# New tokens' attention woven into the last convolution tiles, another buffer layout at the merge gates, and the residual's gates at the output projection

## The chip, the cores and the metric

The kernel runs on one core of one Trainium2 chip. The metric is the device time of one execution in microseconds, as the median of several runs; lower is better. Names of the engines: PE is TensorE (matrix products), DVE is VectorE, ACT is ScalarE, POOL is GpSimd, and SP is SyncE, which issues all of this kernel's transfers from one queue.

## What is computed

One layer of a decoder for a prompt of 1024 tokens and for 8 new tokens ("samples") with a cache of 256 tokens each. Cut to what matters here:

```
h = RMSNorm(x) * g_pre * (1 + scale) + shift
z = h @ w_in                       # one projection for both mixers
ya = (attention(z) * silu(za)) @ w_br_a
yb = (cb * conv3(cc * cx) * silu(cg)) @ w_br_b
ga, gb = sigmoid(merge)            # the merge gates, 2 x 1024 columns of z
o  = (ga * ya + gb * yb) @ w_out
y  = x + gate * RMSNorm(o) * g_post
```

`attention` has three branches with own keys and values (compressed, selected, window) and a gate on each. `gate` is the residual's gate, a vector per request from `w_ada`. All data are float32.

## The kernel before

Nearly every product is made of three PE passes, high part by high part, high by low and low by high (`mm`, line 106), where the low part is the value less its rounded high part (a copy on ACT or DVE, line 110 or 112, and a subtraction on DVE or POOL, line 115). Tokens lie in the free dimension: TT = 1032 columns (1024 of the prompt and 8 new ones), in 3 tiles of CH = 344 columns. The model's 1024 rows are 8 tiles of 128. Weights come through a ring `W` of three raw buffers (`wraw`) and three split ones (`wh`, `wl`).

The order of the code is the order of priority; a scheduler then orders each engine's instructions, and every engine runs its list strictly in that order. A tile of a closed pool gives its memory to the pools opened behind it on the same side ("left" or "right"), and a write to such memory waits for the last reader of what lay there, transfers included.

The stages from the middle on, with the names that matter:

- The prompt's attention (up to line 1108), with three of the four convolution tiles as filler between its products.
- The fourth convolution tile (`conv_tiles(3, ...)`, line 1120): four projections of 72 products each (cc, cx, cb, cg), evaluated by DVE, ACT and POOL.
- Branch B's projection (`w_br_b`, the loop from line 1299): 8 x 3 tiles of 12 products with 344 columns. Into it the generator `sample_steps` is woven, two steps a tile. It is the new tokens' attention: for each of the two branches over cached keys, 8 samples are loaded (`skv`), transposed on PE (`psT<-ident,skv`), split by ACT and DVE (`skT`), multiplied with the queries (`psS<-skT,qd`), put through a softmax, and multiplied with the cached values in 16 products of 8 columns (`psO<-sPT,skv`; each is two records in the trace). The same loop also makes sums of `Hh`, `Hl` for the merge gates (`sums23`).
- The `za` projection (line 1338): its end `e_za` makes `zt`, then `oh` and `ol`, which are stored to `oad` in HBM.
- The merge gates (line 1364 on): pairs of column tiles by a seven-product scheme (`a11`, `a12`, `s2`, `s3`, `s1`, `a22`, `s4`), whose weights are loaded into six buffers `ra`, summed on DVE (`wraw`), split, and multiplied. `M` receives branch B's result again (`M<-ybd`).
- Branch A's projection (`w_br_a`, loop at line 1583): 8 x 3 tiles of 12 products; DVE joins each tile with its gate (`sg`, `M`, lines 1597 and 1598). Beside it `w_out` is loaded (`wor`) and split into `WOh` (ACT) and `WOl` (half on DVE, half on POOL). After the third column tile the function `residual_gates` is called (line 1600).
- The output projection: 8 token tiles of 48 products with 512 columns, `split_m` ahead of each and `finish` behind it.

Of the kernel before, what the change touches and what calls it, by code (L numbers as in the profile page):

```python
# [29 lines left out]
NS = 8  # L30
# [55 lines left out]
def _build(ctx, tc, nc, I, O):  # L86
# [27 lines left out]
    def sub(eng, out, a, b):  # L114
        eng.tensor_tensor(out=out, in0=a, in1=b, op=OP.subtract)  # L115
# [998 lines left out]
    bctx = ExitStack()  # L1114
    bp = pool("bp", "right", bctx)
    YH = bp.tile([128, 4, TT], F32R, name="YH")
    YL = bp.tile([128, 4, TT], F32R, name="YL")
    zctx = ExitStack()
    zp = pool("zp", "left", zctx)
    y3 = zp.tile([128, TT], F32, name="y3")  # L1120
    conv3 = conv_tiles(3, y3, zp)
    for n, _ in enumerate(conv3):
        if n % 24 == 8 and n // 24 < 3:
            f = n // 24
            copy(A, YH[:, f, :], YB[f])
            sub(V, YL[:, f, :], YB[f], YH[:, f, :])
    copy(A, YH[:, 3, :], y3)
    sub(V, YL[:, 3, :], y3, YH[:, 3, :])
    pt = bank("T")
    for f in range(4):  # L1130
        PE.transpose(pt[:10, 128 * f:128 * f + 128], ucs[:, f, :], ident)
    csr = zp.tile([10, 512], F32, name="csr")
    copy(V, csr, pt[:10])
    dma(O["conv_state_prompt"][0, 0], csr[0:2, :])
    dma(O["conv_state_sample"][0, :, 1, :], csr[2:10, :])
    zctx.close()
    yctx.close()
    dram = ctx.enter_context(tc.tile_pool(name="dram", bufs=1, space=bass.MemoryType.DRAM))
    gm_d = dram.tile([18, D], F32, name="gmd")
    oa_d = [dram.tile([3, 128, 4, CH], F32, name=f"oad{i}") for i in range(2)]  # L1140
    sg_d = dram.tile([KT, 128, TT], F32, name="sgd")
    yb_d = dram.tile([KT, 128, TT], F32, name="ybd")


    HT, HS = TT // 2, TT // 4
    tsctx = ExitStack()
    tsp = pool("tsp", "left", tsctx)
    T2, T3 = ([tsp.tile([128, 4, HT], F32R, name=f"T{i}{x}") for x in "hl"] for i in (2, 3))

    def add(out, a, b):  # L1150
        V.tensor_tensor(out=out, in0=a, in1=b, op=OP.add)

    def quarter(k, c):

        cs = slice(HT * c, HT * c + HT)
        return Hh[:, k, cs], Hl[k][:, cs]

    def two(h, l, src):
        copy(A, h, src)
        sub(V, l, src, h)  # L1160

    def sums23(tp):
        for k in range(4):
            for s in range(2):
                cs = slice(HS * s, HS * s + HS)

                def part(k, c):
                    return [x[:, cs] for x in quarter(k, c)]

                a, b = (tp.tile([128, HS], F32, name=x, tag=x, bufs=1) for x in ("ta", "tb"))  # L1170
                add(a, *part(k + 4, 1))
                add(b, *part(k, 1))
                sub(V, a, a, b)
                two(T3[0][:, k, cs], T3[1][:, k, cs], a)
                yield
                add(b, *part(k, 0))
                add(b, a, b)
                two(T2[0][:, k, cs], T2[1][:, k, cs], b)
                yield


    sctx = ExitStack()
    sp = pool("smp", "left", sctx)
# [105 lines left out]

    def branch_mm(acc, w, Xh, Xl, cs):  # L1290
        wh, wl = w
        for k in range(4):
            mm(acc, wh[:, k, :], Xh[:, k, cs], k == 0, False)
            mm(acc, wh[:, k, :], Xl[:, k, cs], False, False)
            mm(acc, wl[:, k, :], Xh[:, k, cs], False, k == 3)

    steps = sample_steps()
    making = sums23(sp)
    for f in range(KT):
        w = W.get()  # L1300
        for c in range(3):
            acc = bank("acc" if (3 * f + c) % 5 < 2 else "S")[:, :CH]
            cs = slice(c * CH, (c + 1) * CH)
            branch_mm(acc, w, YH, YL, cs)
            yb = sp.tile([128, CH], F32, name="yb", tag="yb", bufs=2)
            copy(A, yb, acc)
            dma(yb_d[f, :, cs], yb)
            next(steps, None)
            next(steps, None)
            if f > 1:  # L1310
                next(making, None)
        W.release()
    for _ in steps:
        pass
    sctx.close()
    bctx.close()
# [5 lines left out]
    tp = pool("tp", "left", tctx)  # L1322
    t1 = tp.tile([128, 4, HT], F32, name="t1")

# [13 lines left out]
    for j in range(4):  # L1338
        def e_za(c, acc, cs):
            t = tp.tile([128, CH], F32, name="zt", tag="zt", bufs=3)  # L1340
            oh = tp.tile([128, CH], F32R, name="oh", tag="oh", bufs=2)
            ol = tp.tile([128, CH], F32R, name="ol", tag="ol", bufs=2)
# [22 lines left out]
    gp = pool("gsp", "left", gctx)  # L1365

# [8 lines left out]
    class Pair:  # L1375
# [63 lines left out]
        def after(self, x, s, ps):  # L1439
            def tmp(name, bufs=2):  # L1440
                return gp.tile([128, HS], F32, name=name, tag=name, bufs=bufs)
# [26 lines left out]
        def end(self, i, c, s, z):  # L1468

            f, cs = self.f + i, slice(HT * c + HS * s, HT * c + HS * s + HS)  # L1470
            if self.gb:
                t = gp.tile([128, HS], F32, name="ct", tag="ct", bufs=5)
                A.activation(t, z, AF.Tanh, scale=0.5)
                V.scalar_tensor_tensor(M[:, f, cs], t, 1.0, M[:, f, cs], op0=OP.add, op1=OP.mult)
                return
            if i == 0 and c == 0 and s == 0:
                self.sg = [gp.tile([128, TT], F32, name="sgo", tag="sgo", bufs=2) for _ in range(2)]
                self.left = [4, 4]
# [4 lines left out]

    gm = gp.tile([18, D], F32, name="gm")
# [75 lines left out]
    def residual_gates():  # L1560
        gm = op_.tile([19, D], F32, name="gm2")
        dma(gm[0:18, :], gm_d)
        dma(gm[18:19, :], I["b_ada"][:, 2048:3072])
        gs2 = op_.tile([51, D], F32R, name="gs2")
        kr = op_.tile([51, 136], F32R, name="kr")
        V.memset(f32(gs2), 0.0)
        copy(V, kr, ksel[:, 9:145])
        copy(A, gs2[0:19, :], gm)
        sub(V, gs2[32:51, :], gm, gs2[0:19, :])
        gps = op_.tile([128, D], F32, name="gps")  # L1570
        src = I["g_post"]
        dma(gps, bass.AP(tensor=src.tensor, offset=src.offset, ap=[[0, 128], [1, D]]))
        V.tensor_scalar(gps, gps, float(D) ** 0.5, None, op0=OP.mult)
        for b in range(2):
            cs = slice(512 * b, 512 * b + 512)
            ps = bank("T")
            mm(ps, kr[:, 0:128], gs2[:, cs], True, True)
            V.tensor_tensor(out=GG[:, cs], in0=ps, in1=gps[:, cs], op=OP.mult)
            ps = bank("T")
            mm(ps[:NS, :], kr[:, 128:136], gs2[:, cs], True, True)  # L1580
            V.tensor_tensor(out=GS[:, cs], in0=ps[:NS, :], in1=gps[:NS, cs], op=OP.mult)

    for f in range(KT):
        sg = op_.tile([128, TT], F32, name="sg", tag="sg", bufs=3)
        dma(sg, sg_d[f])
        for h in range(2):
# [4 lines left out]
            sub(P if h else V, WOl[f][:, cs], r, WOh[:, f, cs])  # L1591
# [8 lines left out]
        if f == 2:  # L1600
            residual_gates()
# [48 lines left out]

    mt, xt = {}, {}
# [25 lines left out]
    split_m(0)  # L1677
    for t in range(8):
# [44 lines left out]
```

## Time and profile before

| | |
|---|---|
| median of 3 runs (lowest to highest) | 1083.23 us (1078.26 to 1083.63) |
| the profiled execution | 1082.31 us, its span 1080.5 us |
| mean granted clock of PE over the span | 0.976 of full speed |
| busy share of the span | PE 96%, DVE 67%, ACT 50%, POOL 10% |
| DMA | 104.16 MB, 96 GB/s over the span |
| chain that ended last | PE 76%, DVE 10%, DMA 4%, ACT 4%, rest 6% |

The span runs from the first to the last instruction; what lies around it is the 1.8 us between the two times of the profiled execution. Since PE is busy nearly throughout, its busy share alone tells little: what is to be looked for are stretches in which it waits or in which its granted clock is below 1.00. Matmul records overlap, so the distance between two starts is what a product costs, and not its length.

### The profile page before, as it was taken

The numbers are of one execution on the slowest core, as the hardware profiler recorded it, in microseconds if no ns is written. First come the engines' busy times: TensorE is split into PE (matmuls) and PEld (weight loads), VectorE is DVE, ScalarE is ACT, GpSimd is POOL, SyncE is SP. The second block draws the span as 40 slices with busy tenths as digits, with TensorE's granted clock in tenths as the row PEclk, the third lists the DMA queues.
The fourth block names the chain that finished last, engine by engine and source line by source line (L and its number), as shares of the span: only waits on it lengthen the run. The fifth ranks groups of instructions, "written<-read, shape, count | busy, mean of one in ns | idle before, by whom it ended". The sixth has DMA issues, their size and how long they took to land.

```text
span 1080.5 us, 18059 instructions
## 1 busy us (share of the span) xinstructions
PE 1033.0 (96%) x6526; PEld 950.1 (88%) x6526; DVE 729.0 (67%) x1912; ACT 545.3 (50%) x1198; POOL 105.4 (10%) x106
## 2 busy tenths in 40 slices
PE   5899999999999999999999999998999999999997
PEld 4689999988888889988999989997899999988786
DVE  4676755368877988878878485294656676794433
ACT  4566533358888877887775042232344444222221
POOL 2100000122221211211110000000000000121000
PEclk9999999989999999999999998898999999999999
DMA  9753243211110101111002226335734423773222
GB/s 322 220 143 90 71 101 79 70 35 39 28 30 16 30 15 26 25 25 26 12 18 79 72 92 209 107 112 187 244 109 119 118 69 113 245 226 99 79 79 78
DMA packets 117179, 104.16 MB, mean 96 GB/s; under 512 B 25443, under 2 KB 101674, under 8 KB 117090
## 3 DMA queue, kind: packets, MB, share of 16 engines
q1 hardware_dynamic: 117090, 103.02, 32.3%
q8 instruction: 51, 0.84, 0.3%
q14 instruction: 38, 0.31, 0.1%
HBM read 79.13 MB, written 21.76 MB: 93 GB/s over the span
## 4 chain that ended last, share of the span: by engine, by line
PE 76%; DVE 10%; DMA 4%; ACT 4%; issue 2%; SPq 1%; POOL 1%; POOLq 0%; DVEq 0%; ACTq 0%
PE psacc L106 35%; PE psS L106 22%; PE psO L106 6%; PE psT L1016 5%; PE psT L106 5%; DVE P L961 2%; DVE P L987 2%; ACT P L966 1%; SPq L91 1%; DVE pl L115 1%; DMA sg<-sgd 1%; ACT ph L110 1%; PE psT L1028 1%; DMA ar<-w_ada 1%; DVE sm L975 1%
## 5 line engine op out<-in xcount | busy, mean ns | idle before, releaser
L106 PE MATMUL psacc<-Hh,wh 128*128 128x344 f32 (+1 forms) x816 | 261.7, 321 | 8.9 <-ACT c L110 5.0
L106 PE MATMUL psacc<-Hl,wh 128*128 128x344 f32 (+1 forms) x816 | 258.6, 317 | 0.8 <-DVE ss L329 0.6
L106 PE MATMUL psacc<-Hh,wl 128*128 128x344 f32 (+1 forms) x816 | 258.1, 318 | 0.1
L106 PEld LDWEIGHTS psacc<-Hh,wh 128*128 128x128 f32 x816 | 155.1, 190 | 17.1 <-ACT c L110 5.2
L106 PEld LDWEIGHTS psacc<-Hl,wh 128*128 128x128 f32 x816 | 154.9, 190 | 5.7 <-DVE Hl L115 2.2
L106 PEld LDWEIGHTS psacc<-Hh,wl 128*128 128x128 f32 x816 | 154.5, 190 | 2.4 <-DVE wl L115 1.1
L966 ACT ACTIVATE P<-P,mx 128x64 f32<-128x64 f32 (+5 forms) x192 | 115.1, 600 | 34.7 <-DVE mx L961 32.9
L115 DVE TENSOR_TENSOR pl<-psT,ph 128x512 fp32r<-128x512 f32 x132 | 90.4, 687 | 24.6 <-ACT ph L110 24.1
L110 ACT ACTIVATE wh<-wraw 128x512 fp32r<-128x512 f32 x94 | 58.9, 627 | 79.7 <-PE psS L106 37.0
L1016 PE MATMUL psT<-ident,P 128*128 128x128 f32 x528 | 89.5, 280 | 9.3 <-DVE P L987 7.1
L115 DVE TENSOR_TENSOR wl<-wraw,wh 128x512 fp32r<-128x512 f32 x98 | 67.3, 688 | 41.2 <-ACT wh L110 39.5
L110 ACT ACTIVATE ph<-psT 128x512 fp32r<-128x512 f32 x132 | 77.9, 591 | 28.6 <-PE psT L1016 24.5
L961 DVE CUSTOM_DVE_ANT_0 P<-psS,kbig 128x64 f32<-128x64 f32 (+4 forms) x192 | 74.2, 407 | 20.2 <-PE psS L106 19.4
L1016 PEld LDWEIGHTS psT<-ident,P 128*128 128x128 f32 x528 | 63.6, 141 | 26.9 <-DVE P L987 10.9
L106 PE MATMUL psS<-K,qh 128*128 128x384 f32 (+6 forms) x208 | 67.7, 328 | 2.0 <-DMA qh<-qh 1.1
L106 PE MATMUL psS<-K,ql 128*128 128x384 f32 (+6 forms) x208 | 68.5, 330 | 0.0
L115 POOL TENSOR_TENSOR wl<-wraw,wh 128x512 fp32r<-128x512 f32 x28 | 37.1, 1325 | 275.0 <-ACT wh L110 262.9
L106 PE MATMUL psO<-pl,V 128*128 128x512 f32 x132 | 60.7, 460 | 0.0
L106 PE MATMUL psO<-ph,V 128*128 128x512 f32 x132 | 52.4, 397 | 0.0
L961 DVE CUSTOM_DVE_ANT_0 P<-psS,kbig,mx 128x256 f32<-128x256 f32 (+3 forms) x80 | 41.9, 524 | 9.3 <-PE psS L106 8.3
L115 POOL TENSOR_TENSOR WOl<-wor,WOh 128x512 fp32r<-128x512 f32 x8 | 11.6, 1445 | 342.2 <-ACT WOh L110 338.2
L106 PEld LDWEIGHTS psS<-K,qh 128*128 128x128 f32 x208 | 39.6, 190 | 4.8 <-DMA qh<-qh 1.4
(393 smaller groups left out, 2374.3 us busy)
## 6 DMA issues: line engine op xcount, KB each, us to landing
wraw<-w_in SPq DMA_DIRECT2D x46, 256.0 KB
ra<-w_in SPq DMA_DIRECT2D x32, 256.0 KB
ybd<-yb SPq DMA_DIRECT2D x24, 172.0 KB
M<-ybd SPq DMA_DIRECT2D x8, 516.0 KB
sgd<-sgo SPq DMA_DIRECT2D x8, 516.0 KB
OA<-oad SPq DMA_DIRECT2D x6, 688.0 KB
sg<-sgd SPq DMA_DIRECT2D x8, 516.0 KB
x<-x_prompt SPq DMA_DIRECT2D x8, 512.0 KB
```

Of the source, the lines that this page charges most:

```text
L91: return nc.sync.dma_start(out, in_)
L106: PE.matmul(out, lhsT, rhs, start=start, stop=stop, skip_group_check=True)
L110: A.activation(out, in_, AF.Copy)
L115: eng.tensor_tensor(out=out, in0=a, in1=b, op=OP.subtract)
L961: V.tensor_tensor_reduce(out=Pb[:, j, o:o + n], in0=ps[:, c0:c0 + n], in1=m, scale=1.0, scalar=init, op0=OP.add, op1=OP.min, accum_out=mx[ ...
L966: A.activation(Pb[:, j, 0:total_n], Pb[:, j, 0:total_n], AF.Exp, bias=mx[:, j, ci % 2:ci % 2 + 1], scale=-1.0, accum_out=sm[:, 0, x, j:j + 1])
L975: V.tensor_tensor(out=fac, in0=fac, in1=gt_[:, b0:b0 + np_, :], op=OP.mult)
L987: V.tensor_scalar(p, p, f[:, jj:jj + 1], None, op0=OP.mult)
L1016: PE.transpose(pt[:, j * 128:(j + 1) * 128], u.P[u.br][:, j, n * 128:(n + 1) * 128], ident)
L1028: PE.transpose(pt[:64, j * 128:(j + 1) * 128], u.P[0][:, j, :], ident)
```

## The change

1. `sample_steps` is defined ahead of the fourth convolution tile, and its pool moves to the right side. One step runs at every fourth yield of the convolution's projections (24 of its 39 parts); the rest runs in branch B's loop, one step a tile instead of two.
2. At the merge gates, the buffers `oh`, `ol` and `zt` of the `za` projection are placed first in their pool, and the gate pool places `gm`, `sgo`, `c1`, `u2`, `u3`, `ct` first and `ra` behind them, so that other buffers lie over each other.
3. `residual_gates` is called behind `split_m(0)` at the output projection, and its tiles lie in that stage's pool.
4. All low parts of `w_out` are made on DVE.

```diff
@@ the fourth convolution tile @@
-    bctx = ExitStack()
...
     sctx = ExitStack()
-    sp = pool("smp", "left", sctx)
+    sp = pool("smp", "right", sctx)
...
+    steps = sample_steps()
+    bctx = ExitStack()
...
     for n, _ in enumerate(conv3):
+        if n % 4 == 3:
+            next(steps, None)
         if n % 24 == 8 and n // 24 < 3:
...
@@ branch B @@
-    steps = sample_steps()
-    making = sums23(sp)
+    t23ctx = ExitStack()
+    tp = pool("tp23", "left", t23ctx)
+    making = sums23(tp)
...
             dma(yb_d[f, :, cs], yb)
             next(steps, None)
-            next(steps, None)
...
@@ za @@
     tp = pool("tp", "left", tctx)
+    zt = {x: [tp.tile([128, CH], d, name=x, tag=x, bufs=b) for _ in range(b)] for x, d, b in
+          (("oh", F32R, 2), ("ol", F32R, 2), ("zt", F32, 3))}
     t1 = tp.tile([128, 4, HT], F32, name="t1")
...
@@ merge gates @@
     gp = pool("gsp", "left", gctx)
+    gm = gp.tile([18, D], F32, name="gm")
+    fresh = {"sgo": [gp.tile([128, TT], F32, name="sgo", tag="sgo", bufs=2) for _ in range(2)]}
+    for x, b in (("c1", 2), ("u2", 2), ("u3", 2), ("ct", 5)):
+        fresh[x] = [gp.tile([128, HS], F32, name=x, tag=x, bufs=b) for _ in range(b)]
...
@@ branch A @@
-            sub(P if h else V, WOl[f][:, cs], r, WOh[:, f, cs])
+            sub(V, WOl[f][:, cs], r, WOh[:, f, cs])
...
-        if f == 2:
-            residual_gates()
...
@@ output projection @@
     def residual_gates():
-        gm = op_.tile([19, D], F32, name="gm2")
+        gm = ob.tile([19, D], F32, name="gm2")
...
     split_m(0)
+    residual_gates()
     for t in range(8):
```

What this does to the order of the instructions is shown at three places.

PE, the products of the new tokens' probabilities with the cached values (`psO<-sPT,skv`) of the first branch. Before, in branch B's loop (`YH`, `YL` are branch B's operands):

```order
L106 MATMUL psacc<-YH,wl 128x344
L106 MATMUL psO<-pn,vnew 128x64
L106 MATMUL psO<-sPT,skv 128x8 x16
L106 MATMUL psacc<-YH,wh 128x344
L106 MATMUL psacc<-YL,wh 128x344
```

Now, in the fourth convolution tile (12 products with 344 columns lie between this group of four and the next, and so on up to the fourth):

```order
L106 MATMUL psacc<-Hh,wl 128x344
L106 MATMUL psO<-pn,vnew 128x64
L106 MATMUL psO<-sPT,skv 128x8 x4
L106 MATMUL psacc<-Hh,wh 128x344
L106 MATMUL psacc<-Hl_280,wh 128x344
...
L106 MATMUL psacc<-Hh,wl 128x344
L106 MATMUL psO<-sPT,skv 128x8 x4
L106 MATMUL psacc<-Hh,wh 128x344
```

The sixteen products that stood in one run now stand in four groups; the second branch's, which stood in two groups of eight within branch B's loop, stand in four there as well.

SP, the first loads of the merge gates, with what each waits for (`DMAHW` with a number is one of eight counters of transfers, used in turn). Before:

```order
L91 DMA M<-ybd 128x1032 [waits DMAHW5_49]
L91 DMA ra<-w_in 128x4x128 [waits DMAHW6_49]
L91 DMA ra<-w_in 128x4x128 [waits DMAHW2_49,DMAHW7_49,DMAHW0_49,Pool_49]
L91 DMA ra<-w_in 128x4x128
L91 DMA ra<-w_in 128x4x128 [waits DMAHW1_49]
```

Now:

```order
L91 DMA M<-ybd 128x1032 [waits DMAHW5_49]
L91 DMA ra<-w_in 128x4x128 [waits DMAHW6_49,PE_49]
L91 DMA ra<-w_in 128x4x128 [waits DMAHW7_49]
L91 DMA ra<-w_in 128x4x128 [waits DMAHW0_49]
L91 DMA ra<-w_in 128x4x128 [waits DMAHW1_49]
```

The loads stand at the same place of the queue. The second no longer waits for counter 2, which belongs to the last store of `oh` (`oad<-oh`) three rows ahead of the first of these loads.

PE, the residual's gates (`psT<-gs,kr`). Before, in branch A's loop (`OA` is its operand):

```order
L106 MATMUL psT<-gs_11034,kr 128x512
L106 MATMUL psT<-gs_11034,kr 8x512
L106 MATMUL psS<-OA_10675,wl 128x344
L106 MATMUL psT<-gs_11034,kr 128x512
L106 MATMUL psT<-gs_11034,kr 8x512
L106 MATMUL psS<-OA_10761,wh 128x344
```

Now, in the second token tile of the output projection:

```order
L106 MATMUL psS<-WOh,mh 128x512
L106 MATMUL psT<-gs_11356,kr 128x512
L106 MATMUL psT<-gs_11356,kr 8x512
L106 MATMUL psS<-WOl_10836,mh 128x512
...
L106 MATMUL psS<-WOl_10837,mh 128x512
L106 MATMUL psT<-gs_11356,kr 128x512
L106 MATMUL psS<-WOh,ml 128x512
L106 MATMUL psS<-WOh,mh 128x512
L106 MATMUL psT<-gs_11356,kr 8x512
```

The four products, which nothing but one product of branch A parted, now stand apart between products of the output projection, behind its first token tile.

## Rows read from the trace of the kernel before

**Rows 1.** Windows of 5 us in branch B's loop: length, engines' busy time (instructions), PEclk, DMA share, GB/s.
```profile
630.00:635.00 5.00, 5.00 (x35) 4.74 (x34) 4.55 (x14) 2.40 (x7) 0.00 (x0) 1.00 0.41 135
...
650.00:655.00 5.00, 5.00 (x31) 4.24 (x29) 4.01 (x12) 1.45 (x4) 0.00 (x0) 0.84 0.53 135
655.00:660.00 5.00, 5.00 (x23) 5.00 (x23) 0.00 (x0) 0.00 (x0) 0.00 (x0) 0.50 0.81 283
660.00:665.00 5.00, 5.00 (x24) 4.94 (x23) 2.60 (x8) 0.84 (x2) 0.00 (x0) 0.63 0.96 312
...
680.00:685.00 5.00, 5.00 (x37) 4.72 (x35) 0.69 (x2) 1.37 (x3) 0.00 (x0) 0.92 0.70 190
685.00:690.00 5.00, 5.00 (x21) 5.00 (x21) 0.42 (x2) 0.00 (x0) 0.00 (x0) 0.50 0.10 35
690.00:695.00 5.00, 5.00 (x30) 5.00 (x30) 1.12 (x2) 1.09 (x3) 0.00 (x0) 0.90 0.11 35
```

**Rows 2.** Chain that ended last, fourth convolution tile and branch B: start, length, engine, tile, line.
```profile
581.89 41.16 PE psacc L106 x262
...
652.11 6.37 PE psO L106 x34
...
684.14 3.08 PE psO L106 x16
```

**Rows 3.** Timeline of PE around products of 8 columns: start, length, instruction.
```profile
680.98 1.95 PE L106 MATMUL psO<-sPT,skv 128*128 128x8 f32 x16
682.79 0.40 PE L106 MATMUL psS<-YH,wl 128*128 128x344 f32 x1
683.03 0.32 PE L106 MATMUL psS<-YH,wh 128*128 128x344 f32 x1
```

**Rows 4.** Instructions on tile `skT`: shortest, median and longest in ns, first and last start.
```profile
L110 ACT ACTIVATE skT<-psT x16: 376/385/390, 633.8 to 674.8; 128x256 fp32r<-128x256 f32 x16
L115 DVE TENSOR_TENSOR skT<-psT,skT x16: 410/418/425, 634.4 to 675.3; 128x256 fp32r<-128x256 f32 x16
```

**Rows 5.** Timeline of DVE at the fourth convolution tile's start.
```profile
583.57 1.23 DVE L115 TENSOR_TENSOR YL<-YB,YH 128x1032 fp32r<-128x1032 f32 x1
```

**Rows 6.** Chain that ended last, from `za` into the merge gates.
```profile
746.78 4.02 DMA oad<-oh
...
751.37 5.32 DMA ra<-w_in
```

**Rows 7.** Timeline of SP (its DMA queue) at the same place.
```profile
747.71 1.00 SPq L91 DMA_DIRECT2D M<-ybd  x2
748.76 5.94 SPq L91 DMA_DIRECT2D ra<-w_in  x6
```

**Rows 8.** Timeline of ACT and a window (columns as in rows 1) at the same place.
```profile
751.45 0.66 ACT L110 ACTIVATE c<-psacc 128x258 f32<-128x258 f32 x2 [4.69 <-DMA oad<-ol]
...
750.00:755.00 5.00, 3.11 (x14) 3.11 (x15) 0.00 (x0) 0.79 (x3) 0.00 (x0) 0.50 1.09 369
```

**Rows 9.** Timeline of PE in branch A around the residual's gates; in brackets idle time and releaser.
```profile
952.27 0.48 PE L106 MATMUL psS<-OA,wh 128*128 128x344 f32 x2
952.98 0.73 PE L106 MATMUL psT<-gs,kr 51*128 51x512 f32 x2 [0.23 <-DVE gs L115]
...
957.38 0.94 PE L106 MATMUL psS<-OA,wh 128*128 128x344 f32 x2 [1.91 <-DVE sg L1597]
...
960.84 0.48 PE L106 MATMUL psacc<-OA,wh 128*128 128x344 f32 x2
```

**Rows 10.** Groups of DVE's instructions in branch A (925 to 978 us): busy, mean ns, idle before.
```profile
L115 DVE TENSOR_TENSOR WOl<-wor,WOh 128x512 fp32r<-128x512 f32 x8 | 5.5, 684 | 1.2 <-ACT WOh L110 1.1
```

**Rows 11.** Timelines of POOL, DVE and ACT in branch A.
```profile
949.10 1.49 POOL L115 TENSOR_TENSOR WOl<-wor,WOh 128x512 fp32r<-128x512 f32 x1 [4.41 <-ACT WOh L110]
...
949.36 1.52 DVE L112 CAST wh<-wraw 128x512 fp32r<-128x512 f32 x1
...
966.18 0.63 ACT L110 ACTIVATE WOh<-wor 128x512 fp32r<-128x512 f32 x1 [3.94 <-DMA wor<-w_out]
```

More of the change, by code (lines that the diff above doesn't have):

```diff
@@ L1111, in _build @@
     att.close()
-    bctx = ExitStack()
[L1115 to L1179, printed above, removed]
@@ L1288, in sample_steps @@
                  os_[r].rearrange("p (s h) -> p s h", h=8)[:, :, 4 * g:4 * g + 4])
+    steps = sample_steps()
+    bctx = ExitStack()
+    bp = pool("bp", "right", bctx)
+    YH = bp.tile([128, 4, TT], F32R, name="YH")
+    YL = bp.tile([128, 4, TT], F32R, name="YL")
+    zctx = ExitStack()
+    zp = pool("zp", "left", zctx)
+    y3 = zp.tile([128, TT], F32, name="y3")
+    conv3 = conv_tiles(3, y3, zp)
+    for n, _ in enumerate(conv3):
+        if n % 4 == 3:
+            next(steps, None)
+        if n % 24 == 8 and n // 24 < 3:
+            f = n // 24
+            copy(A, YH[:, f, :], YB[f])
+            sub(V, YL[:, f, :], YB[f], YH[:, f, :])
@@ new lines, in _build @@
+    copy(A, YH[:, 3, :], y3)
+    sub(V, YL[:, 3, :], y3, YH[:, 3, :])
+    pt = bank("T")
+    for f in range(4):
+        PE.transpose(pt[:10, 128 * f:128 * f + 128], ucs[:, f, :], ident)
+    csr = zp.tile([10, 512], F32, name="csr")
+    copy(V, csr, pt[:10])
+    dma(O["conv_state_prompt"][0, 0], csr[0:2, :])
+    dma(O["conv_state_sample"][0, :, 1, :], csr[2:10, :])
+    zctx.close()
+    yctx.close()
+    dram = ctx.enter_context(tc.tile_pool(name="dram", bufs=1, space=bass.MemoryType.DRAM))
@@ new lines, in _build, with add @@
+    gm_d = dram.tile([18, D], F32, name="gmd")
+    oa_d = [dram.tile([3, 128, 4, CH], F32, name=f"oad{i}") for i in range(2)]
+    sg_d = dram.tile([KT, 128, TT], F32, name="sgd")
+    yb_d = dram.tile([KT, 128, TT], F32, name="ybd")
+    HT, HS = TT // 2, TT // 4
+    tsctx = ExitStack()
+    tsp = pool("tsp", "left", tsctx)
+    T2, T3 = ([tsp.tile([128, 4, HT], F32R, name=f"T{i}{x}") for x in "hl"] for i in (2, 3))
+    def add(out, a, b):
+        V.tensor_tensor(out=out, in0=a, in1=b, op=OP.add)
@@ new lines, in quarter, with two, sums23, part @@
+    def quarter(k, c):
+        cs = slice(HT * c, HT * c + HT)
+        return Hh[:, k, cs], Hl[k][:, cs]
+    def two(h, l, src):
+        copy(A, h, src)
+        sub(V, l, src, h)
+    def sums23(tp):
+        for k in range(4):
+            for s in range(2):
+                cs = slice(HS * s, HS * s + HS)
+                def part(k, c):
+                    return [x[:, cs] for x in quarter(k, c)]
+                a, b = (tp.tile([128, HS], F32, name=x, tag=x, bufs=1) for x in ("ta", "tb"))
+                add(a, *part(k + 4, 1))
+                add(b, *part(k, 1))
+                sub(V, a, a, b)
+                two(T3[0][:, k, cs], T3[1][:, k, cs], a)
+                yield
+                add(b, *part(k, 0))
+                add(b, a, b)
+                two(T2[0][:, k, cs], T2[1][:, k, cs], b)
+                yield
@@ L1314, in _build @@
         pass
+    t23ctx.close()
+    bctx.close()
     sctx.close()
-    bctx.close()
     tsp4 = pool("tsp4", "left", tsctx)
@@ L1322, in _build, with spare @@
     tp = pool("tp", "left", tctx)
+    zt = {x: [tp.tile([128, CH], d, name=x, tag=x, bufs=b) for _ in range(b)] for x, d, b in
+          (("oh", F32R, 2), ("ol", F32R, 2), ("zt", F32, 3))}
     t1 = tp.tile([128, 4, HT], F32, name="t1")
+    def spare(name, dtype, bufs):
+        return zt[name].pop(0) if zt[name] else tp.tile([128, CH], dtype, name=name, tag=name, bufs=bufs)
     def sums14():
@@ L1440, in tmp @@
             def tmp(name, bufs=2):
-                return gp.tile([128, HS], F32, name=name, tag=name, bufs=bufs)
+                return gtile(name, HS, bufs)
             def total(a, b):
@@ L1471, in end @@
             if self.gb:
[L1472 removed]
+                t = gtile("ct", HS, 5)
                 A.activation(t, z, AF.Tanh, scale=0.5)
@@ L1476, in end @@
             if i == 0 and c == 0 and s == 0:
-                self.sg = [gp.tile([128, TT], F32, name="sgo", tag="sgo", bufs=2) for _ in range(2)]
+                self.sg = [gtile("sgo", TT, 2) for _ in range(2)]
                 self.left = [4, 4]
```

51 lines of the change are left out of this document (25 added, 26 removed).

## The prediction

> **What bounds the kernel now.** Four views were read, in this order. The page says that PE is busy 96% of the span and carries 76% of the chain that ended last, so a change can gain only where PE stands or runs at a lower granted clock. The windows over the span came next: PEclk is below 1.00 in a few places, and two of them lie in branch B's loop, where PE does not stand at all [rows 1]. The chain of waits then gives the price of one product and names what held PE at the merge gates [rows 2, 6]. Last, the timelines around these places show which instruction the engines were held by [rows 3, 5, 7 to 9, 11].
>
> One price serves throughout: 262 products of 344 columns took 41.16 us, so one costs 0.157 us at the full clock [rows 2].
>
> **Part A, the new tokens' attention.** In branch B's loop the granted clock was 1.00 while transposes, small products and large ones were mixed (630 to 635), fell to 0.50 in 655 to 660, and again in 685 to 690; PE was busy 5.00 of 5 us throughout [rows 1]. That is the lower of the two levels, 1.2 in place of 2.4 GHz. What PE did just before each fall is in the chain: 34 records of 6.37 us from 652.11, and 16 of 3.08 us from 684.14, all products of 8 columns on `psO` [rows 2]. So I read runs of these tiny products as what lowers the clock. The cost: in each window of 5 us the work lost is 5 x (1 - PEclk), that is 0.80 + 2.50 + 1.85 for the first fall and 0.40 + 2.50 + 0.50 for the second, together 8.55 us [rows 1].
>
> The change takes the first run of 34 records apart into four groups of 8, with 12 large products between them, and the second branch's two runs of 16 likewise. A group of 8 takes about 8 x 0.113 = 0.9 us (16 records began at 680.98 and the next product at 682.79), ahead of 12 x 0.157 = 1.88 us of large products [rows 2, 3]. That looks like the mixture of 630 to 635, which kept 1.00 [rows 1]. I therefore take the whole 8.55 us as gained. Against it stand the breaks between the two kinds of product: the first large product behind a run lasted 0.24 us to the next start, against 0.157, so a break costs about 0.08 us on that side and, by estimate, as much on the other; eight groups in place of three runs are 5 more, at 0.2 us 1.0 us [rows 3]. Net 7.5 us. The bounds: nothing of the clock comes back and the breaks remain, -1; all of it and no price for breaks, 9.
>
> What is only moved and costed at nothing: 24 of 39 steps with their loads, transposes and copies. PE's products are as many as before. The loads of cached keys and values leave SP's queue some 40 us earlier; in 655 to 665 the queue ran at a DMA share of 0.81 to 0.96 and PE still did not stand [rows 1], so weights of the convolution should not come late. The cover of a step is the 12 large products between its transposes and the products that need them, 1.88 us; ACT's 0.385 and DVE's 0.418 us for `skT` make 0.80 of it [rows 4], which leaves 1.08 us for what stands ahead of them on DVE. If that cover is gone, PE stands before each step (the last rival).
>
> The Trainium skill, page "TensorE: Matmul & The Clock Gate", section "Why this matters for your kernels", says that drops of throughput in the middle of a kernel come from idle stretches of PE between bursts of products, and to keep PE fed. By that rule alone the clock should not have fallen at 655, where the trace has no idle time, and rearranging busy work would return nothing. The row differs from it, and the row decides; what the sum would be by the rule is the first rival's 1078.0.
>
> **Part B, the merge gates.** The chain ran through the store `oad<-oh` (from 746.78, 4.02 us) and then the load of `ra` from 751.37 [rows 6]. The second `ra` load waited for that store, since it overlaid `oh`; SP's queue had the first at 748.76, right behind the loads of `M` [rows 7]. In the new layout that wait is gone, and the second load could leave at about 749.2 instead of 751.37: 2.2 us. But in 750 to 755 the DMA share was already 1.09, so an earlier issue partly shares the same bandwidth [rows 8]. ACT's copy `c`, which waited 4.69 us for the other store, no longer waits, but PE was held by `ra` for longer, so this alone gives nothing [rows 6, 8]. The bounds are 0 and 2.2; I take 1.6, nearer the issue time, because the store's wait ended the chain.
>
> **Part C, branch A and the output projection.** Ahead of the residual's gates, two products of branch A began at 952.27, so the next would have begun at 952.59. From there to the product at 960.84 lie 13 products of branch A; at 0.157 us they end at 954.6, and 6.2 us were lost [rows 2, 9]. In them are two short pairs of the residual's own products, a stand of 1.91 us for DVE's `sg`, and a stretch at the lower clock behind it, where two products last 0.94 instead of 0.48 us [rows 9]. The four products do not vanish: at 0.73 us a pair they cost 1.5 us at the output projection [rows 9], where their operands have a whole token tile of products as cover. That leaves 4.7 us.
>
> The low parts of `w_out` go the other way. POOL's half took 1.49 us for one, and a DVE cast beside it 1.52 [rows 11], against 0.684 us for DVE's own subtraction of the same size [rows 10]. On DVE the other half adds 8 x 0.684 = 5.5 us of work, and it stands in DVE's queue behind `WOh`, whose 8 present waits cost 1.2 us [rows 10]; `WOh` itself stood 3.94 us for `wor` [rows 11]. What is queued behind such a wait is the join of a tile with its gate, for which PE has already been seen to wait. DVE also loses the residual's own operations here and the stretching by POOL, so I charge PE only 1.0 us, close to the 1.2 of the present half. Net 3.7 us; the bounds are 0 (all of it goes to waits for DVE) and 5.5 (4.7 plus the smaller stretch of DVE's casts).
>
> **The sum.** 7.5 + 1.6 + 3.7 = 12.8 us off the profiled execution's 1082.3 (span 1080.5 and 1.8 around it) is 1069.5. The median of the runs shown is 1083.2, 0.9 above that execution.
>
> **The rivals.**
> - *The clock falls all the same.* If any mixture with tiny products lowers it, the first part gives -1.0 and the time is 1082.3 + 1.0 - 1.6 - 3.7 = 1078.0; if only one of the two passages falls, about 1074. For it: the fall came with PE fully busy, so I cannot show from one kernel how many tiny products are too many. Against: 630 to 635 stood at 1.00 with transposes between the large products [rows 1]. Chance 0.18: 0.10 for both, 0.08 for one.
> - *DVE becomes the bound of branch A.* With all low parts behind `wor` and `WOh` on one engine in strict order, `sg` and the weights' casts come late and part C gives nothing: 1073.2. For it: the waits of 1.2 and 3.94 us [rows 10, 11]. Against: DVE loses the residual's work. Chance 0.08.
> - *The loads at the merge gates are limited by bandwidth.* The share of 1.09 speaks for it [rows 8]; the chain's wait for a store against it [rows 6]. Part B gives 0: 1071.1. Chance 0.06.
> - *Slower: PE stands before the keys' products in the convolution.* DVE works strictly in order, and there it also has the convolution's own work, such as `YL` with 1.23 us [rows 5]. From 1.08 us of queue ahead of `skT` on, PE stands; with 2.3 us ahead at each of 16 steps [rows 4] it is 16 x 1.2 = 19.2 us, and the time 1088.7. For it: one `YL` alone exceeds the margin. Against: there are three of them for 16 steps, and in 630 to 635, with DVE busy 4.55 of 5 us, PE did not stand [rows 1]. Chance 0.07.
>
> **How the numbers follow.** The forecast keeps 0.61. A measurement of this kernel can tell about 0.5%, 5.4 us, from no change. Faster by more (below 1077.8): the forecast, the one-passage case, the second and third rival, 0.83, less 0.02 for smaller gains of several parts at once, 0.81. Within: both passages fall, 0.10, and those 0.02, with 0.01 of the slower rival in weak form, 0.13. Slower: 0.06. The range of 8 in 10 goes from 1064 (9 + 2.2 + 5.5 would be 1065.6, with 1.6 for the scatter between runs) up to 1078, which takes in three of the rivals and the edge of the first.
>
> **What would show it.** Right: PEclk at 1.00 in every window of the convolution's last tile and branch B; records on `psO` in groups of 8 and none at twice the length; no idle time of PE ahead of `psS<-skT`; the second `ra` load right behind the first; no stand at `psT<-gs` and no lower clock around it in branch A; the same products at the output projection without a wait. Wrong: PEclk of 0.50 again behind the groups of tiny products; PE waiting for DVE's `skT` in the convolution; PE waiting for `sg` or `wl` while DVE waits for `WOh`; the first seven-product group starting as late as before.

## The result and the profile after

The changed kernel takes **1070.85 us** (median of 4 runs, 1070.16 to 1071.64) against 1083.37 for the kernel before (4 runs, 1078.26 to 1083.63). The ratio is 0.9894, with a 95% interval of 0.9868 to 0.9920. The profiled execution took 1071.21 us, its span is 1069.2 us, and PE's mean granted clock rose from 0.976 to 0.986. The forecast was 1069.5.

So that the parts can be judged apart, the span is cut at starts of PE's products that every kernel has: the last `psO<-pl,V` of the prompt's attention, the last product with `YH` or `YL` (end of branch B), the first `psS<-T2h` (the first `s2`), the first with `OA` (branch A), the first `WOh,wh` and the last with `WO` (output projection). In us, profiled executions:

| stretch | before | after | difference |
|---|---|---|---|
| fourth convolution tile and branch B | 117.01 | 108.02 | -8.99 |
| `za`, up to the first `s2` | 60.64 | 61.36 | +0.72 |
| merge gates | 166.43 | 167.12 | +0.69 |
| branch A | 52.52 | 45.40 | -7.12 |
| output projection | 96.31 | 98.92 | +2.61 |

The stretch ahead of these came out 0.7 us longer in this one execution, and what lies behind the last product is unchanged; together they make the 11.4 us between the two spans (1080.54 and 1069.17 us).

Windows of the changed kernel around the places where the small products now stand (columns as in [rows 1]):

```profile
620.00:625.00 5.00, 5.00 (x38) 5.00 (x37) 0.36 (x1) 0.00 (x0) 0.00 (x0) 1.00 0.75 207
625.00:630.00 5.00, 5.00 (x38) 5.00 (x38) 0.51 (x1) 0.46 (x1) 0.93 (x1) 1.00 0.87 277
...
660.00:665.00 5.00, 5.00 (x35) 4.45 (x33) 3.58 (x11) 1.30 (x4) 0.00 (x0) 1.00 0.36 105
665.00:670.00 5.00, 5.00 (x38) 5.00 (x38) 3.96 (x10) 1.94 (x5) 0.00 (x0) 1.00 0.49 126
```

The number to read is PEclk, the third from the end: it is 1.00 in all of them, and in every other window of 5 us from 580 to 740, where [rows 1] had 0.50 twice. PE was busy 5.00 of 5 us in these windows and in those; its busy share alone could not have told the two apart. PE does not wait for `skT` anywhere from 582 to 690, but it stands 1.3 us there for branch B's operand `YH` and the probabilities `sP` (total in us, times, longest), where the kernel before has one stand of 0.3:

```profile
PE psacc L106 <- ACT YH L110: 0.7, 1, 0.7
PE psT L1161 <- DVE sP L1155: 0.6, 2, 0.4
```

The instructions on the tile `psO` of the changed kernel (shortest, median and longest in ns, first and last start) say the same of the products themselves:

```profile
L106 PE MATMUL psO<-sPT,skv x64: 170/256/277, 619.3 to 671.0; 128*128 128x8 f32 x64
```

None is as long as those that ran at the lower clock before (median 361 ns there). The chain that ended last, at the merge gates (start, length, engine, tile, line), answers to [rows 6]:

```profile
738.82 1.73 PE psacc L106 x12
...
741.71 7.43 DMA ra<-w_in
...
751.30 0.80 PE psS L106 x2
```

The wait for the store `oad<-oh` is gone from the chain, as intended, but the load of `ra` behind it now takes 7.43 us from its issue, where it took 5.32. SP's queue shows what stands ahead of it:

```profile
738.51 0.32 SPq L91 DMA_DIRECT2D oad<-oh  x1
739.07 0.32 SPq L91 DMA_DIRECT2D oad<-ol  x1
739.44 1.01 SPq L91 DMA_DIRECT2D M<-ybd  x2
740.54 6.59 SPq L91 DMA_DIRECT2D ra<-w_in  x6
```

As before [rows 7], the six loads of `ra` stand right behind loads of `M`, of 516 KB each. What PE waits for from 725 on (total in us, times, longest) and the windows at the place:

```profile
PE psS L106 <- ACT wh L110: 9.3, 1, 9.3
PE psacc L106 <- ACT c L110: 0.2, 1, 0.2
```

```profile
740.00:745.00 5.00, 1.97 (x17) 1.75 (x15) 0.00 (x0) 0.66 (x2) 0.00 (x0) 1.00 0.99 349
745.00:750.00 5.00, 0.00 (x0) 0.00 (x0) 0.80 (x2) 0.00 (x0) 0.00 (x0) 0.65 1.19 306
750.00:755.00 5.00, 3.70 (x17) 3.70 (x18) 3.97 (x7) 1.75 (x3) 0.00 (x0) 0.50 0.89 256
755.00:760.00 5.00, 5.00 (x37) 5.00 (x37) 3.01 (x7) 0.91 (x2) 0.00 (x0) 0.82 0.77 267
```

Before, PE stood 5.0 us for ACT's `c` and 2.1 for `wh`, with the products of `a12` between. Now `c` comes at once, `a12` runs at once, and the whole wait is one stand of 9.3 us, after which PE begins again at 0.50.

That list of waits holds nothing from branch A: no `sg`, no `gs`, no `GG`. The chain there is PE's alone:

```profile
918.58 3.87 PE psacc L106 x24
922.45 5.69 PE psS L106 x36
928.14 3.76 PE psacc L106 x24
...
960.20 3.78 PE psS L106 x24
```

24 products in 3.76 to 3.78 us is the full rate of 0.157 each, where [rows 9] had a stand and a stretch at the lower clock. DVE's groups between 918 and 964 show what it carries for that (busy, mean ns, idle before; the sixteenth subtraction lies just behind the stretch):

```profile
L115 DVE TENSOR_TENSOR WOl<-wor,WOh 128x512 fp32r<-128x512 f32 x15 | 10.2, 688 | 2.3 <-ACT WOh L110 2.3
```

Its waits for `WOh` doubled with the number of subtractions, from 1.1 [rows 10] to 2.3 us, and PE waited for none of it.

### The profile page after: what moved, and what is told of

It is laid out like the page before. It is cut to its first block, busy times and chain, and to the rows that moved or that the text cites. A ratio compares the mean times of both kernels' runs of the same rounds, so it can differ in the third digit from the quotient of the medians.

```text
span 1069.2 us, 18057 instructions
## 1 busy us (share of the span) xinstructions
PE 1021.5 (96%) x6526; PEld 940.3 (88%) x6526; DVE 727.9 (68%) x1920; ACT 545.6 (51%) x1198; POOL 94.0 (9%) x98
## 4 chain that ended last, share of the span: by engine, by line
PE 77%; DVE 10%; ACT 4%; issue 2%; DMA 1%; SPq 1%; POOL 1%; POOLq 0%; DVEq 0%; ACTq 0%
PE psacc L106 36%; PE psS L106 23%; PE psO L106 6%; PE psT L106 5%; PE psT L1016 5%; DVE P L961 2%; DVE P L987 2%; ACT P L966 1%; DVE pl L115 1%; SPq L91 1%; DMA ra<-w_in 1%; ACT ph L110 1%; PE psT L1028 1%; DVE sm L975 1%; PE psT L570 1%
## 5 line engine op out<-in xcount | busy, mean ns | idle before, releaser
L1613 POOL TENSOR_TENSOR fst<-fst,mhalf 128x1 f32<-128x1 f32 (+1 forms) x9 | 4.9, 549 | 422.5 <-DVE fst L1612 422.5
```

The source lines that it names most:

```text
L1613: P.tensor_tensor(out=st[:n, 3:4], in0=st[:n, 3:4], in1=mhalf[:n], op=OP.pow)
```

## The experiments

All are compared with the kernel before, run beside them on the same chip; its median there was 1081.7 to 1082.4. The columns are the stretches of the table above, from the profiled execution.

| kernel | median, us | ratio to before (95%) | conv., B | to `s2` | gates | A | output |
|---|---|---|---|---|---|---|---|
| only A | 1071.22 | 0.9896 (0.9872 to 0.9920) | 108.04 | 60.53 | 165.00 | 51.92 | 96.31 |
| only B | 1082.40 | 1.0002 (0.9989 to 1.0015) | 117.01 | 60.48 | 166.61 | 49.60 | 96.31 |
| only C | 1078.55 | 0.9970 (0.9958 to 0.9982) | 116.96 | 60.68 | 166.52 | 45.37 | 98.92 |
| C, low parts half on POOL | 1078.24 | 0.9963 (0.9948 to 0.9979) | 117.01 | 61.06 | 166.28 | 45.78 | 98.92 |
| A and C | 1070.60 | 0.9905 (0.9876 to 0.9933) | 108.03 | 60.66 | 164.93 | 46.53 | 98.91 |
| one run a branch | 1073.12 | 0.9917 (0.9892 to 0.9943) | 110.72 | 60.84 | 166.41 | 45.72 | 98.91 |
| two runs a branch | 1068.03 | 0.9877 (0.9851 to 0.9903) | 107.52 | 60.56 | 166.07 | 45.40 | 98.92 |
| spread only | 1079.45 | 0.9974 (0.9959 to 0.9990) | 115.80 | 60.52 | 164.97 | 52.09 | 96.31 |
| `M` late | 1066.50 | 0.9862 (0.9836 to 0.9888) | 108.04 | 56.73 | 166.18 | 45.68 | 98.92 |
| `M` late, old order of B | 1066.73 | 0.9863 (0.9846 to 0.9881) | 108.04 | 57.03 | 164.89 | 45.73 | 98.98 |
| `M` late, two runs, other pool | 1066.94 | 0.9875 (0.9857 to 0.9892) | 107.52 | 57.13 | 166.33 | 46.14 | 99.45 |
| `M` late, two runs, `ra` in `M` | 1066.96 | 0.9852 (0.9830 to 0.9873) | 112.23 | 56.66 | 167.19 | 45.39 | 98.91 |

### One part at a time

The edits are the hunks of the change, by part: A the convolution and branch B, B `za` and the merge gates, C branch A and the output projection.

**Only A.** 

> Only part A (new tokens' attention begun in the fourth convolution tile), merge gates, branch A and output projection as before. Theory: part A is worth what the trace of the changed kernel gave between the end of the prompt's attention and the start of za, 8.3 to 9.0 us, whatever the other parts do: about 1074.7 us, PEclk 1.00 in every window of branch B's loop, and the stand at the merge gates as before (4.98 and 2.09 us of PE). Rival: part of that gain comes from the new buffer order (shorter queues behind it), then A alone gives clearly less than 7.5 us: above 1076.

The stretch is 8.97 us shorter, the same as in the whole change, but the run is 3.5 us faster than expected: 1071.2. In the profiled execution PE's second stand at the merge gates was 1.2 us (2.1 before), and the gates were 1.4 us shorter. The windows show that the clock was back by 750 and stayed:

```profile
740.00:745.00 5.00, 2.12 (x10) 2.12 (x11) 0.00 (x0) 0.66 (x2) 0.00 (x0) 0.72 1.04 378
745.00:750.00 5.00, 3.77 (x19) 3.47 (x18) 2.36 (x4) 1.81 (x4) 0.00 (x0) 0.59 1.19 310
750.00:755.00 5.00, 5.00 (x42) 4.81 (x41) 4.84 (x10) 1.36 (x3) 0.00 (x0) 1.00 0.95 290
```

Before, the clock had come back and fell once more:

```profile
755.00:760.00 5.00, 2.91 (x18) 2.59 (x17) 3.16 (x5) 2.40 (x5) 0.00 (x0) 0.84 1.08 293
760.00:765.00 5.00, 5.00 (x33) 5.00 (x33) 3.60 (x8) 0.63 (x1) 0.00 (x0) 0.73 0.96 312
```

Branch A is 0.6 us shorter, with 2.1 us of stands in place of 3.2; the stand of 1.9 us for `sg` is still there. So part A alone is as fast as the whole change (1071.22 against 1070.85), as far as the intervals can tell.

**Only B.** 

> Only part B (buffer order at za and the merge gates). Theory: the loads at the merge gates are held by the DMA engines and not by the wait for the store, so the first product of s2 comes 0.7 us later behind the last oad<-oh (12.8 instead of 12.1 us) and PE, which now stands in one piece of 9.3 us, starts again at the lower clock and loses some 0.7 us more; branch A gets back up to 1 us since the loads of sg no longer wait for the store of gm. In all between 1082 and 1085, no gain to be told. Rival (the prediction's own step): s2 starts 1.6 us sooner, 1081.8.

1082.4: no difference. `s2` began neither later nor 1.6 us sooner (60.48 against 60.64), so both theories missed its start by size; the chain shows the load of `ra` at 6.69 us from its issue where the kernel before had 5.32. The 2.9 us less in branch A belong to this execution, in which the clock stayed at 1.00 behind the stand for `sg`; the medians are equal.

**Only C.** 

> Only part C (residual's gates at the output projection, all low parts of w_out on DVE). Theory: branch A runs without a stand (24 products in 3.76 to 3.78 us throughout), which is 7.2 us sooner at the output projection, and that stage is 2.7 us longer (2.0 for the residual's products in three places, 0.7 for products of 512 columns at 0.2334 in place of 0.2313 us): 4.5 us, 1078.9. Rival: part of branch A's gain belongs to part B, because sg's loads still wait for the store of gm here; then PE stands for sg or OA in branch A, and the gain is 2.5 to 3.5 us, 1080 to 1081.

1078.55, as the theory had it: in the profiled execution branch A is 7.15 us shorter and the output projection 2.61 longer. PE waits for nothing in branch A although the buffer order is the old one, so the rival falls.

**The move of the residual's gates without the other half of C.** The edit to the run before:

```diff
-            sub(V, WOl[f][:, cs], r, WOh[:, f, cs])
+            sub(P if h else V, WOl[f][:, cs], r, WOh[:, f, cs])
```

> Only the move of the residual's gates; the low parts of w_out stay half on POOL. Theory: the move alone takes away the stand at psT<-gs and sg, the split on POOL costs only DVE's stretched operations, which branch A can hide: within 1 us of the run with both (about 1079 to 1080), the output projection again 2.7 us longer. Rival: POOL's subtractions are what makes DVE late in branch A; then PE still waits for sg or wl there and the gain is under 2 us, 1081.5 or more.

1078.24, and branch A 45.78 in place of 45.37: which engine makes the low parts is worth 0.4 us at most and nothing in the median. The gain of C is the move.

**A and C.** 

> Parts A and C without B. Theory: B is a loss once A is there; without it the start of s2 and the gates take what the run with A alone showed (60.5 and 165.0 us in place of 61.4 and 167.1), and branch A and the output projection what the run with C alone showed (45.4 and 98.9 us): about 3 us under the changed kernel, 1067 to 1068. Rival: the 2.9 us belong to a chance of the one profiled run (the clock recovering in time or not), and A and C together are the changed kernel's time, 1070 to 1071.

The profiled execution is 1.9 us under that of the changed kernel, but the median, 1070.60, is the same: B is worth nothing that can be told, with A or without it. The 2 us at the gates are again the clock coming back sooner, as with only A; the profiled execution is the fastest of the four, which went from 1069.19 to 1073.85 (the changed kernel's from 1070.16 to 1071.64). C, too, is worth less behind A than alone. From only A to A and C, branch A is 5.4 us shorter and not 7.15: 0.6 had gone with A already, and PE stands 0.9 us for `OA` here. Less the 2.6 at the output projection this is 2.8 us, but the medians differ by 0.6 (1071.22 and 1070.60), and their intervals, of some 3 us to each side, allow either.

### What lowered the clock

**One run a branch.** In `sample_steps`:

```diff
-                if s % 2:
+                if s == NS - 1:
                     yield
```

> The changed kernel, but the 16 products of 8 columns of a branch stand again in one run (32 records) in place of four groups of 8 records; everything else stays where the change put it. Theory: it is the run that lowers the clock. PEclk falls to 0.50 behind the run in the convolution and behind the one in branch B's loop, at some 5 us each as at 650 to 665 before, less 1.2 us for six breaks fewer: 1079 to 1080. Rival: the fall belonged to the place in branch B's loop (or to its loads), not to the run; then PEclk stays 1.00 and the time is 1069.7 to 1071.

1073.12 us, some 6 less than expected, but the clock fell behind each of the two runs (34 records in the chain: 32 of 8 columns and two of 64):

```profile
619.16 4.03 PE psO L106 x34
...
657.19 4.03 PE psO L106 x34
```

```profile
620.00:625.00 5.00, 5.00 (x39) 5.00 (x39) 0.49 (x1) 0.00 (x0) 0.00 (x0) 0.93 0.70 226
625.00:630.00 5.00, 5.00 (x25) 5.00 (x25) 0.66 (x3) 0.46 (x1) 0.23 (x1) 0.73 0.90 301
...
660.00:665.00 5.00, 5.00 (x27) 5.00 (x28) 2.73 (x8) 0.67 (x2) 0.00 (x0) 0.68 0.00 0
665.00:670.00 5.00, 5.00 (x33) 5.00 (x32) 3.79 (x10) 1.77 (x6) 0.00 (x0) 0.98 0.46 125
```

So the run does it, in the convolution as in branch B; the rival falls. But the loss is 0.35 + 1.35 + 1.60 + 0.10 = 3.4 us where the same two branches lost 8.55 before. The run alone, in this place, does not bring back the whole of part A.

**Spread only.** The kernel before, with one line more:

```diff
                 if s % 2:
                     yield
+                    yield
```

> The kernel before, with nothing moved into the convolution, but two yields behind every four products of 8 columns. The order that comes of it: the second branch's products stand in four groups of 8 records with 8 to 12 large products between them; the first branch's in one group of 24 records and, 12 large products later, one of 8. Theory: spreading is what keeps the clock, not the place. Behind the second branch PEclk stays 1.00 (3.4 us of 8.55 gained); behind the group of 24 it falls or not, which no run has shown yet: 1079 if it falls, 1074 if not. Rival: work that is short of large products in branch B's loop lowers the clock wherever the small ones stand; then both falls are there again and the time is 1082.

1079.45 us. Behind the first group (24 records) PE ran at 0.50 throughout 655 to 665. The second branch, for which the theory had 1.00, still lost 0.45 + 1.25:

```profile
655.00:660.00 5.00, 5.00 (x21) 5.00 (x22) 0.20 (x1) 0.19 (x1) 0.00 (x0) 0.50 0.69 193
660.00:665.00 5.00, 5.00 (x21) 5.00 (x21) 3.76 (x9) 0.88 (x2) 0.00 (x0) 0.50 0.39 142
...
685.00:690.00 5.00, 5.00 (x33) 4.71 (x33) 1.33 (x3) 0.88 (x2) 0.00 (x0) 0.91 0.29 77
690.00:695.00 5.00, 5.00 (x28) 5.00 (x28) 0.00 (x0) 0.46 (x1) 0.00 (x0) 0.75 0.42 110
```

What stood ahead of that second fall is in the chain:

```profile
685.70 1.35 PE psO L106 x10
687.05 1.37 PE psacc L106 x8
688.42 0.79 PE psO L106 x8
689.21 3.53 PE psacc L106 x12
```

The stretch gains 1.2 us of the 9. So groups of 8 records do not keep the clock by themselves. Two things differ from the changed kernel: the steps still come two a tile, so the transposes and the small products ahead of each group are as dense as before, and 8 large products lie between these two groups and not 12. Which of them it is was not tried. Taken with the run before: thinner steps with the runs kept gave 117.01 - 110.72 = 6.3 us (5.1 of it clock), spread groups in dense steps 1.2, both together 9.0.

**Two runs a branch.** The edit `if s % 4 == 3: yield`, groups of 16 records.

> As the run before, but two groups of 8 products (16 records each, some 1.8 us) with 12 products of 344 columns (1.9 us) between them. One reading: groups of 16 are what fell at 684 before, so the clock falls here too, behind the second group at the least: 1075 to 1078. Other reading: at 684 it was the short distance of 7 large products between the two groups; with 12 between them the clock stays 1.00 and the time is 1070 to 1071.

1068.03 us, under both readings. With 12 large products between the groups the clock stayed 1.00 and the stretch took 107.52: 0.50 us less than with four groups. Nearly all of this is PE's stands, 0.9 us in place of 1.3:

```profile
PE psacc L106 <- ACT YH L110: 0.6, 1, 0.6
PE psT L1161 <- DVE sP L1155: 0.3, 1, 0.3
```

With the stands taken out, four breaks fewer save 0.4 us in the large products, and the products of 8 columns cost 0.3 us more, so a break costs next to nothing. In the profiled executions the rest of the gain lies where the edit changes nothing (0.9 us ahead of these stretches, 0.8 up to `s2`, 1.1 at the gates).

That the clock stayed is luck, as the later run with the same groups (`ra` in `M`, below) shows. Its chain and windows:

```profile
656.95 2.24 PE psO L106 x18
659.19 2.78 PE psS L106 x12
661.97 3.21 PE psO L106 x16
665.19 6.27 PE psacc L106 x24
```

```profile
655.00:660.00 5.00, 5.00 (x35) 4.37 (x35) 4.25 (x13) 0.88 (x2) 0.00 (x0) 1.00 0.33 96
660.00:665.00 5.00, 5.00 (x24) 5.00 (x23) 0.00 (x0) 0.77 (x2) 0.00 (x0) 0.51 0.23 62
665.00:670.00 5.00, 5.00 (x18) 5.00 (x19) 3.63 (x10) 1.18 (x3) 0.00 (x0) 0.50 0.00 0
```

The second branch's products in the same order lost 5 us in that execution, and none in the two other kernels that group them so. The steps are thin there, and the loss is larger than the 3.4 us of both whole runs above; so neither the length of a group nor the density of the steps tells alone how long the clock stays low.

### The loads at the merge gates

**`M` late.** Each load of `M` waits for a column copied from the current pair's `c1`:

```diff
                 for f in range(2 * p.n - 4, 2 * p.n - 2):
+                    copy(V, M[:, f, 0:1], p.c1[0][:, 0:1])
                     dma(M[:, f, :], yb_d[f])
```

> The changed kernel, with each of the loads M<-ybd made to wait for the pair of gates in whose place it is written (one column of its tile is first copied from that pair's c1), so that no load of M lies ahead of the first loads of ra. Theory: the stand of 9.3 us at s2 is DMA time, three loads of 516 KB being ahead of ra; without them ra lands about 5 us sooner, and PE stands 4 to 5 us: with less time at the lower clock behind it 1064 to 1066. Rival: ra is limited by its own short rows or by the issue of its loads, and lands within 1 us of now: 1070 to 1071.

1066.5, half a microsecond above the range expected. The load that ends the wait now lands 3.90 us after its issue:

```profile
740.49 3.90 DMA ra<-w_in
...
746.62 3.58 PE psS L106 x15
```

PE's stand fell from 9.3 to 4.7 us and `s2` began 4.6 us sooner. The price of the gates' first loads was the three loads of 516 KB ahead of them, whose rows DVE first read at 841 in the changed kernel, some 100 us after their issue. Whether they delayed `ra` by bandwidth or by their place in the queue was not told apart.

**The old order of B, with `M` late.** 

> Parts A and C with the loads of M held back, but the buffer order of before at za and the merge gates. Theory: B is worth nothing only because three loads of M fill the DMA engines; with these out of the way the wait for the last stores of oh and ol is what ends last, and the old order starts s2 later than the new one did (56.7 us from the end of branch B): 58 to 59.5 us, and the time is 1067.5 to 1069. Rival: the stores land quickly too once M is out of the way and PE's 36 products of a12 fill the wait for ra in either order; then s2 starts at 56.5 to 57 and the time is that of the new order with M held back, 1066 to 1067.

1066.73 against 1066.50, and `s2` at 57.03 against 56.73: the rival was right. Even with the DMA engines free, B changes nothing: what PE gains at `a12` it stands for at `s2`.

**`ra` in `M`.** On top of `M` late and two runs:

```diff
-                self.raw[x] = gp.tile([128, 4, 128], F32, name="ra", tag="ra", bufs=6)
+                self.raw[x] = (gp.tile([128, 4, 128], F32, name="ra", tag="ra", bufs=6) if self.n else
+                               M[:, 4 + 2 * i + kh, 0:512].rearrange("p (k c) -> p k c", k=4))
```

> The changed kernel with M's loads held back, two groups of 8 products per branch, and the first pair's four buffers laid into rows 4 to 7 of M, which are free until the last pairs, instead of ra; so these loads stand ahead of the last stores of oh and ol in SP's queue. Theory: what is left of the stand at s2 (4.7 us) is the landing of these loads, and they start sooner by about 1.5 us: s2 starts 55 to 56 us behind branch B instead of 56.7, the convolution and branch B take 107.5, and the time is 1064 to 1065. Rival: the start is set by the last zt of za, which frees the memory of M as it frees that of ra, and by the DMA engines behind it; then s2 starts at 56.5 to 57 and the time is that of M held back with two groups, 1065.5 to 1066.5.

`s2` began at 56.66: nothing gained, the rival's number. The median is 1066.96, with runs from 1065.31 to 1070.24, of which the profiled one is the slowest, by the 5 us of clock shown above.

### The output projection

**`M` late, two runs, the residual's tiles in the pool of `GG`.** `gm`, `gs2`, `kr` and `gps` are taken from `ggp` and not from `ob`.

> The changed kernel with M's loads held back, two groups of 8 products per branch in place of four of 4, and the residual's tiles in the pool of GG so that the output projection's own buffers lie where they lay before. Theory: the convolution and branch B take 107.5 us (0.5 less, four breaks fewer), s2 starts 56.7 us behind them, and the output projection's products of 512 columns cost 0.2313 us again, since what made them 0.2334 is where the operands lie: 98.3 us in place of 98.9. In all 1065 to 1066. Rival for the last step: the operands' place has nothing to do with it, the output projection stays at 98.9 and the time is near 1066.

The chain's rows of 48 products are the test: first two of this run, then two of the changed kernel, both behind the first token tile's work.

```profile
1001.59 11.12 PE psS L106 x48
1012.71 11.12 PE psacc L106 x48
```

```profile
1006.88 11.21 PE psS L106 x48
1018.09 11.21 PE psacc L106 x48
```

The products of 512 columns are back at 0.2317 us from 0.2336, as the theory had it (0.2313 from 0.2334); where the residual's tiles lie cost the change 0.6 us. The stage as a whole was not shorter (99.45 us, and the time 1066.94 and not 1065 to 1066): with their memory free earlier, the residual's products moved up into the first token tile and PE stood 1.8 us for `GG`.

## Why the prediction was right, and where it was not

The sign, the size and the main mechanism were right; the sum came within 1.4 us, partly since its errors cancel and partly by luck (the second and the last point).

- **Part A: 7.5 predicted, 9.0 measured.** The deficit of 8.55 us in [rows 1] came back in full: all four profiled kernels with the old order took 117.0 us here, all five with thin steps and four groups 108.0, at 1.00 throughout. The 1.0 us charged for five breaks was not due, as the run with two groups shows. The other 0.5 us are mainly the balance of two terms that had been put at nothing. Sorted by kind of product, from start to start, the stretch is shorter by 4.16 us at the products of 8 columns, 3.48 at the large ones, 0.83 at the keys' products (`psS<-skT`) and 0.47 at the transposes of `skv`. The keys' products ran at 1.00 before as well, so their gain is not the clock's; in spread only, with two steps a tile, they and the transposes took as long as before (7.4 us), in the kernel with one run a branch and thin steps as long as after (6.1). Against this PE's stands grew from 0.3 to 1.3 us.
- **What of part A was luck.** The reading that a run of tiny products lowers the clock held. That groups of 8 records would keep it was taken from the window 630 to 635, in which no product of 8 columns stands. They kept it with 12 large products between them and one step a tile, but not in spread only. How long the clock stays low is open: the losses of 8.55 us (old order), 3.4 (one run a branch), 5.1 and 1.7 (spread only, first and second branch) and 5 (two groups of 16, in one execution) follow neither the length of the groups nor the density of the steps alone. The Trainium skill, page "TensorE: Matmul & The Clock Gate", section "Why this matters for your kernels", puts drops of throughput down to idle stretches of PE between bursts. By that rule the clock would have given nothing back here; the trace disagrees, since PE was busy 5.00 of 5 us at 0.50 as well as at 1.00. At the merge gates, where PE does stand, trace and rule agree (0.50 behind the stand of 9.3 us).
- **Part B: 1.6 predicted, 0 measured.** The failed step is "nearer the issue time, because the store's wait ended the chain". The load on the chain (the third of the six, not the second, as I had read it) was issued sooner, behind the last `oad<-oh` by 3.2 us and not 4.6, and took 2.1 us longer, which is the third rival's outcome; holding `M` back showed that the loads of `M` were what it waited behind. The row that said so, a DMA share of 1.09, was read and given too little weight.
- **Part C: 3.7 predicted, 4.5 measured.** Branch A gained 7.1 and not 6.2 less 1.0: it now runs at 45.4 us for 288 products, which at 0.157 would be 45.2. A stand of 0.7 us for `OA` at its start, which the sum did not have, is gone as well, and the charge for DVE's waits was not due, since PE was never behind them. The output projection lost 2.6 and not 1.5: 2.0 for the residual's products, which stand in three places and so pay three times for the change of kind, and 0.6 for the operands' place.
- **The slower rival** was priced by its condition and did not come: PE never waited for `skT`, though DVE was busy 4.94 of 5 us at 590 to 595. **The first rival** (the clock falls all the same) did not come with four groups; the runs with one or two groups, and the groups of 8 in spread only, show that it was near.
- **The sum.** In the profiled executions, -9.0 for A, -4.5 for C, +1.4 at the gates (0.7 at `s2`, 0.7 behind it) and 0.7 ahead of the stretches make the 11.4 us of the two spans. The medians do not bear the sum out part by part: A alone gained 11.2 us, C alone 3.8, A and C 11.5. With A in place, what C adds cannot be told from nothing, nor from the 2.8 us of its stretches. That the forecast met the total is therefore no proof of its third term on top of the first.

The best of these is the changed kernel with `M`'s loads held back: 1066.5 us, ratio 0.9862 (0.9836 to 0.9888) to before; its twin with the old order of B cannot be told from it.

## What to carry to other kernels

A matrix engine that is busy throughout can still run at half its clock: look at the granted clock beside the busy share. If it falls behind a run of small products, thin these out over a longer stretch of large ones; breaking the run alone was not enough here. When a wait for a store is taken away, look at what else is in the queue at that moment; a load that nobody needs yet, standing ahead of the one that is waited for, can cost more than the wait did. A stand that is moved is only a gain if the work behind it does not wait for the same transfer.

## What was not expected of the hardware

- Products of 512 columns took 0.2317 or 0.2336 us each from the third token tile of the output projection on, at the same granted clock of 1.00, according to which other tiles lay in the pool of their operands. Why was not tried.
- The clock's fall is not the same in every execution of one order: the second branch's two groups of 16 records lost 5 us in one kernel's execution and none in two others'.
- At the merge gates in the old order, PE stands twice. In the three profiled kernels whose second stand was 1.6 to 2.4 us (before, only C, C with half on POOL) the clock came back between them and fell again, and the gates took 166.3 to 166.5 us; in the four whose second stand was 1.0 to 1.3 (only A, A and C, spread only, `M` late with the old order) it did not fall again, and they took 164.9 to 165.0. So it went with the second stand in all seven executions; 1.4 us is too little for the medians to tell. Whether the length of the stand or its moment decides, and why it is shorter there, was not tried.
